# One decoder layer in fp32: the first weights in two transfers, and the last block's mean from row sums of the weights

## The chip, the cores and the metric

The kernel runs on one core of a Trainium2 chip. The metric is the device time in microseconds of one execution, as the median of several runs. A core has TensorE (PE, matrix products), VectorE (DVE), ScalarE (ACT), GpSimd (POOL) and SyncE (SP, which issues most transfers here); sixteen DMA engines move data between the chip's memory and the on-chip buffer.

## The reference, cut to what matters

One decoder layer over 256 positions of width 1024: a wide input projection, block-sparse attention (one block of 256 here, so plain causal attention) and a gated short convolution side by side, an output projection, LayerNorm, a feed-forward part with convolution, LayerNorm again.

```python
proj  = x @ w_in                                   # q | k | v | B | C | h | two gates
y_att = attention(rope(q), rope(k), v) @ w_attn_out
y_cnv = (B * causal_dwconv(C * h)) @ w_conv_out
mix   = (sigmoid(g_att) * y_att + sigmoid(g_cnv) * y_cnv) @ w_o
x     = layer_norm(alpha * x + mix)                # alpha = 2 ** 0.25
u     = causal_dwconv(x @ w_up)                    # width 2 * 2816
f     = (silu(u[..., :2816]) * u[..., 2816:]) @ w_down
x     = layer_norm(alpha * x + f)                  # mean, variance, gain and bias over 1024
```

What matters below is the start of the first product (q, k and v) and the end: the second LayerNorm needs the mean and the variance of each row of `alpha * x + f`, where `f` is a product over 2816 = 22 x 128 rows of `w_down`.

## The kernel before

All products are made in fp32 by splitting each operand into a high part (rounded to the type that PE takes) and a low part (the rest). A product is three matmuls: high by high, high by low and low by high. ACT makes the high parts with a copy (`wh`), DVE the low parts with a subtraction (`wl`). The 128-row groups of the weights are packed by the host into chunks of up to 2048 columns in the order of use; `issue_dma` brings them with SP into three rotating buffers (`raw`), a chunk as a rule in one transfer. `PIECES` says where a chunk is cut into several. A buffer is free again when both parts of its weights are made.

**Head.** Chunk k (of 8) holds 256 columns of x transposed, then the q, k and v weights of one group of 128 input features: 256 + 1024 + 512 columns. Chunk 0 comes in four transfers: x, q weights, k weights, v weights (`PIECES[0]`), chunk 1 in two. While they are under way, PE runs 36 small products of zeros (`warm_up`). Then DVE alone makes the high and the low part of x (L574, L575) and the high part of the q weights (L577), PE runs the products of pass 0 (high by high) and pass 2 (low x by high weights) for each half of the positions, DVE makes the low q weights (L579), and pass 1 follows. The k weights (`split_part(1, 1, 2)`) and the v weights (`split(2)`) follow, each on ACT for the high part and on DVE for the low part. From then on `qkv_split` works ahead by up to two chunks. All matmuls of this stage have line L568.

**Middle.** PE runs through the layer without a break; `slot` places the work of ACT and DVE beside each product by hand: first the ACT steps due, then the high parts of the weights some units ahead (`split_h`, L192), then the low parts (`split_l`, L197), then the DVE steps due. Each engine takes its instructions in the order in which they are written.

**Tail.** `down` adds the product of f group i with its 128 rows of `w_down` to four accumulators `dacc[t][nh]` (two blocks of 128 positions, two halves of 512 columns; L305 to L307). The last 8 of the 22 groups (`TAIL`) are left over to the end. `finish(0)` runs them for block 0, then DVE adds the residual, takes the statistics (`residual`, L779 and L781), and normalises while PE works on block 1. `finish(1)` runs the 8 groups for the first 512 columns of block 1, then for the third and the fourth quarter of the columns each into a bank of its own (`down_part`, bank `e`). Behind the last product come, on DVE: the add of the fourth quarter (L1012), its statistics (L1013), the aggregate over four pieces (L757), the subtraction of the mean and the product with the gain for two halves (L769), and the product with the inverse deviation plus the bias in two pieces of 640 and 384 columns (L766), each with its output transfer (L1025). POOL makes the inverse deviation by a power (L758).

Of the kernel before, what the change touches and what calls it, by code (L numbers as in the profile page):

```python
# [8 lines left out]
F32 = mybir.dt.float32  # L9
# [6 lines left out]
P = 128  # L16
# [35 lines left out]
PIECES = {0: (0, 256, 768, 1280, 1792), 1: (0, 768, 1792)}  # L52
# [85 lines left out]
def layer_kernel(ctx: ExitStack, tc: tile.TileContext, x, wpack, cpack, ln1_g, ln1_b, ln2_g, ln2_b, out):  # L138
# [49 lines left out]
    def split_h(u):  # L188

        issue_dma(units[u]["chunk"] + RAW_BUFS - 1)  # L190
        alloc(u, "h", "wh")
        nc.scalar.activation(units[u]["h"], raw_of(u), AF.Copy)  # L192

# [42 lines left out]
    warm_up(36)  # L236
# [11 lines left out]
    neghalf2 = cst.tile([P, 1], F32, name="neghalf2")  # L248
    invf = cst.tile([P, 8], F32, name="invf")
# [327 lines left out]
    nc.vector.tensor_copy(wh0[:, 0], w0[:, 0])  # L577
    qkv_passes(0, 0, (0, 1), (0, 2))
# [186 lines left out]
    def norm_second(r, mv, ln, cs):  # L765
        nc.vector.scalar_tensor_tensor(r[:, cs], r[:, cs], mv[:, 3:4], ln[:, 1, cs], op0=ALU.mult, op1=ALU.add)  # L766

    def norm_first(r, mv, ln, cs):
        nc.vector.scalar_tensor_tensor(r[:, cs], r[:, cs], mv[:, 0:1], ln[:, 0, cs], op0=ALU.subtract, op1=ALU.mult)  # L769

# [34 lines left out]
    nc.scalar.activation(neghalf2, neghalf, AF.Silu)  # L805
    banks = [acc_bank(f"o1{nh}") for nh in range(2)]
# [185 lines left out]
    def finish(t):  # L992
        r = x1[:, t]
        stats = tmp.tile([P, 4, 6], F32, tag="stats", name=f"rstats{t}", bufs=2)
        if t == 0:
            for k in range(TAIL):
                down(NP - TAIL + k, (t,))
                slot(tail_from + k, take(2))
            assert not pending
            for nh in range(2):  # L1000
                residual(t, nh, dacc[t][nh], x1, r, stats, nh, nh * 512, nh * 512 + 512)
        else:
            for i in range(NP - TAIL, NP):
                down(i, (t,), (0,))
            nc.vector.scalar_tensor_tensor(r[:, 512:1024], x1[:, t, 512:1024], ALPHA, dacc[t][1], op0=ALU.mult, op1=ALU.add)
            for c in range(2):
                residual(t, 0, dacc[t][0], x1, r, stats, c, c * 256, c * 256 + 256)
            for c in range(2, 4):
                bank = ps_pair(f"e{c}")[:, 0]
                for i in range(NP - TAIL, NP):  # L1010
                    down_part(i, bank, c)
                nc.vector.tensor_tensor(r[:, c * 256:c * 256 + 256], r[:, c * 256:c * 256 + 256], bank[:, 0:256], op=ALU.add)  # L1012
                nc.vector.bn_stats(stats[:, c, :], r[:, c * 256:c * 256 + 256])  # L1013
        mv = norm_stats(r, stats, 2 if t == 0 else 4)
        if t == 0:
            for c in range(2):
                cc = slice(c * 512, (c + 1) * 512)
                norm_apply(r[:, cc], r[:, cc], mv, ln2[:, 0, cc], ln2[:, 1, cc])
                nc.sync.dma_start(out[0, t * P:(t + 1) * P, cc], r[:, cc])
            return  # L1020
        for c in range(2):
            norm_first(r, mv, ln2, slice(c * 512, c * 512 + 512))
        for cc, queue in ((slice(0, 640), nc.sync), (slice(640, D), nc.scalar)):
# [3 lines left out]
    for t in range(2):  # L1027
        finish(t)
# [42 lines left out]
```

## Time and profile before

| | |
|---|---|
| time before, median of 3 runs | 365.47 us (365.17 to 365.59) |
| profiled execution, its own time | 366.63 us |
| span of the profiled execution | 364.6 us |
| granted TensorE clock, mean | 0.997 of full |
| busy: PE / PEld / DVE / ACT / POOL | 355.4 / 306.8 / 297.5 / 226.3 / 16.6 us |
| moved between memory and chip | 69.62 MB, mean 191 GB/s |

A row of the timeline reads: start and duration in us, engine, source line, operation, written tile <- read tiles, sizes, number of instructions that the row merges, and in brackets the idle time of the engine ahead of it with what ended it. PEld is the loading of weights into PE, which overlaps its matmuls; SPq and ACTq are the queues of the engines that issue transfers. In a row of groups the numbers behind the bar are the busy time in us and the mean duration of one in ns, then the idle time ahead of the group. In a row of a stretch, each engine has its busy us and, behind x, the number of instructions that touch the stretch, in the order PE, PEld, DVE, ACT, POOL, then clock, DMA share and GB/s. In a row of transfers stand the number, the size and the median us from issue to landing.

### The profile page before, as it was taken

How to read it: one execution, taken by the hardware profiler on the slowest of the kernel's cores; microseconds unless marked ns; L12 is line 12 of the kernel's file. 1: busy time of each engine (PE TensorE's matmuls, PEld its weight loads, DVE VectorE, ACT ScalarE, POOL GpSimd, SP SyncE). 2: the span in 40 equal slices, each digit the busy share in tenths (PEclk: the TensorE clock that was granted, in tenths of full speed). 3: DMA queues.
4: the chain of work that ended last, by engine and by line, in shares of the span. 5: the costliest groups of instructions: out<-in, count | busy, mean ns of one | idle time of the engine just before them, and what ended most of it. 6: DMA issues, size and time to landing. Idle time of an engine off the chain costs nothing.

```text
span 364.6 us, 5227 instructions
## 1 busy us (share of the span) xinstructions
PE 355.4 (97%) x1956; PEld 306.8 (84%) x1956; DVE 297.5 (82%) x514; ACT 226.3 (62%) x392; POOL 16.6 (5%) x38
## 2 busy tenths in 40 slices
PE   8999999999999999999999999999999999999991
PEld 6788888888898888888888888888888888888891
DVE  4787888779795979989769789987968696999884
ACT  3575876577977966653457566765747476777400
POOL 2000000000000113301100000000000000000000
PEclk9999999999999999999999999999999999999998
DMA  8979565435654453787161835548281735653011
GB/s 259 325 254 338 220 236 184 156 115 201 262 192 150 138 214 134 238 320 299 49 231 39 303 124 229 173 172 309 63 322 53 293 108 239 232 230 117 2 58 58
DMA packets 11241, 69.62 MB, mean 191 GB/s; under 512 B 1232, under 2 KB 1616, under 8 KB 4176
## 3 DMA queue, kind: packets, MB, share of 16 engines
q1 hardware_dynamic: 10496, 67.00, 50.3%
q0 software_dynamic: 576, 2.10, 1.7%
q8 instruction: 15, 0.25, 0.3%
q10 hardware_dynamic: 144, 0.20, 0.1%
q14 instruction: 10, 0.08, 0.1%
HBM read 68.24 MB, written 1.05 MB: 190 GB/s over the span
## 4 chain that ended last, share of the span: by engine, by line
PE 96%; DMA 1%; DVE 1%; SPq 0%; ACT 0%; DVEq 0%; issue 0%
PE pb L323 20%; PE pb L330 10%; PE g L323 8%; PE d L305 5%; PE d L306 5%; PE d L307 5%; PE g L330 4%; PE y L323 4%; PE v L568 3%; PE q L568 3%; PE k L568 3%; PE b L323 2%; PE y L330 2%; PE c L323 2%; PE o L305 2%; PE o L307 2%
## 5 line engine op out<-in xcount | busy, mean ns | idle before, releaser
L197 DVE TENSOR_TENSOR wl<-raw,wh 128x1024 fp32r<-128x1024 f32 x99 | 121.0, 1225 | 25.3 <-ACT wh L192 25.1
L192 ACT ACTIVATE wh<-raw 128x1024 fp32r<-128x1024 f32 x99 | 103.7, 1054 | 32.2 <-DMA raw<-in_wpack 32.2
L323 PE MATMUL pb<-x1T,wh 128*128 128x512 f32 x320 | 76.2, 390 | 0.0
L323 PEld LDWEIGHTS pb<-x1T,wh 128*128 128x128 f32 x320 | 59.7, 188 | 12.1
L330 PEld LDWEIGHTS pb<-x1T,wl 128*128 128x128 f32 x320 | 41.0, 191 | 1.6
L330 PE MATMUL pb<-x1T,wl 128*128 128x256 f32 x320 | 41.5, 283 | 0.0
L220 DVE TENSOR_TENSOR wl<-raw,wh 128x1024 fp32r<-128x1024 f32 (+1 forms) x29 | 27.3, 981 | 7.5 <-ACT wh L219 7.3
L323 PE MATMUL g<-xT,wh 128*128 128x512 f32 x128 | 31.7, 395 | 0.0
L305 PE MATMUL d<-wh,f 128*128 128x512 f32 x80 | 31.3, 391 | 0.0
L306 PE MATMUL d<-wl,f 128*128 128x512 f32 x80 | 31.3, 391 | 0.0
L307 PE MATMUL d<-wh,f 128*128 128x512 f32 x80 | 31.1, 389 | 0.0
L219 ACT ACTIVATE wh<-raw 128x1024 fp32r<-128x1024 f32 (+1 forms) x29 | 23.7, 859 | 11.6 <-DMA raw<-in_wpack 7.5
L323 PEld LDWEIGHTS g<-xT,wh 128*128 128x128 f32 x128 | 23.2, 188 | 4.6
L857 DVE SCALAR_TENSOR_TENSOR fc<-fb,consts,fc 128x254 f32<-128x254 f32 x40 | 19.3, 483 | 1.4
L855 DVE SCALAR_TENSOR_TENSOR fc<-fb,consts,fc 128x255 f32<-128x255 f32 x40 | 19.1, 477 | 0.0
L849 ACT ACTIVATE fc<-fb,consts 128x256 f32<-128x256 f32 x40 | 18.0, 497 | 1.4 <-DVE fb L843 1.4
L307 PEld LDWEIGHTS d<-wh,f 128*128 128x128 f32 x80 | 15.0, 188 | 3.2
L305 PEld LDWEIGHTS d<-wh,f 128*128 128x128 f32 x80 | 15.1, 188 | 2.7
L839 ACT ACTIVATE fb<-pb 128x512 f32<-128x512 f32 x20 | 11.8, 592 | 8.7 <-PE pb L330 8.7
L306 PEld LDWEIGHTS d<-wl,f 128*128 128x128 f32 x80 | 15.1, 188 | 2.6
L330 PEld LDWEIGHTS g<-xT,wl 128*128 128x128 f32 x128 | 16.4, 191 | 0.7
L330 PE MATMUL g<-xT,wl 128*128 128x256 f32 x128 | 16.6, 282 | 0.0
(183 smaller groups left out, 580.1 us busy)
## 6 DMA issues: line engine op xcount, KB each, us to landing
raw<-in_wpack SPq DMA_DIRECT2D x55, 1024.0 KB, 5.0
raw<-in_wpack SPq DMA_DIRECT2D x6, 896.0 KB, 6.7
xr<-in_x SPq DMA_DIRECT2D x1, 1024.0 KB, 7.1
ln<-in_ln_g POOLq DMA_DIRECT2D x2, 512.0 KB, 5.7
ln<-in_ln_b POOLq DMA_DIRECT2D x2, 512.0 KB, 6.3
raw<-in_wpack SPq DMA_DIRECT2D x3, 256.0 KB, 3.3
raw<-in_wpack SPq DMA_DIRECT2D x1, 512.0 KB, 6.5
out<-x SPq DMA_DIRECT2D x2, 256.0 KB, 2.0
```

The costliest lines, as they stand in the source:

```text
L192: nc.scalar.activation(units[u]["h"], raw_of(u), AF.Copy)
L197: nc.vector.tensor_tensor(units[u]["l"], raw_of(u), units[u]["h"].bitcast(F32), op=ALU.subtract)
L219: nc.scalar.activation(h, src, AF.Copy)
L220: (eng or nc.vector).tensor_tensor(l, src, h.bitcast(F32), op=ALU.subtract)
L305: nc.tensor.matmul(o, ah, bh, start=start, stop=False)
L306: nc.tensor.matmul(o, ah, bl, start=False, stop=False)
L307: nc.tensor.matmul(o, al, bh, start=False, stop=stop)
L323: nc.tensor.matmul(bank, un["h"][:, k, n0:n0 + P], b[:, k].rearrange("p a s -> p (a s)"), start=k == 0, stop=False)
L330: nc.tensor.matmul(bank[:, 0:S], un["l"][:, k, n0:n0 + P], b[:, k, 0], start=False, stop=k == nk - 1)
L568: nc.tensor.matmul(banks[m][t], (xl if p == 2 else xh)[:, k, t * P:(t + 1) * P], wl if p == 1 else wh, start=k == 0 and p == 0, stop=k == ...
L855: nc.vector.scalar_tensor_tensor(c[:, 1:S], pb[:, a * S:a * S + S - 1], w_ffn(1, j), c[:, 1:S], op0=ALU.mult, op1=ALU.add)
L857: nc.vector.scalar_tensor_tensor(c[:, 2:S], pb[:, a * S:a * S + S - 2], w_ffn(0, j), c[:, 2:S], op0=ALU.mult, op1=ALU.add)
```

## The change

Head: chunk 0 comes in two transfers, x with the q weights (768 columns) and the k with the v weights (1024 columns). The high part of x is made by ACT, at the same time as DVE makes the high q weights; the low part of x follows on DVE. The first products are ordered pass by pass over both halves of the positions. The warm-up has 30 products instead of 36.

Tail: the sum over the columns 768 to 1023 of the last products of block 1 is no longer taken from the products themselves. Each of the last 8 groups of `w_down` gets the sum of its rows over these columns (`rowsum`, an accumulating ACT copy in `split_h`). ACT scales the f groups of block 1 with them (`fs`), POOL adds the eight groups and the two parts up in five steps (`fs_add`; two of them ahead of block 0's power, three behind it), the result is split (`fsr`), and two small products with ones during the fourth quarter (`mean`) sum over the partitions. The other columns are summed by accumulating DVE operations. So the mean is known ahead of the last product. With it ACT squares the first 768 columns (`sq0`, `sq1`), and DVE makes their product with the gain (`res`). Behind the last product come: the add of the fourth quarter to a part from which the mean has been taken, one multiply-and-reduce that completes the variance, the power on POOL beside the product of the last quarter with the gain, and the last operation in two pieces with their output transfers.

```diff
-PIECES = {0: (0, 256, 768, 1280, 1792), 1: (0, 768, 1792)}
+PIECES = {0: (0, 768, 1792), 1: (0, 768, 1792)}
...
+    LAST_UNITS = [U[("dn", i // 2)] + i % 2 for i in range(NP - TAIL, NP)]
+    rowsum = cst.tile([P, TAIL], F32, name="rowsum")
...
         nc.scalar.activation(units[u]["h"], raw_of(u), AF.Copy)
+        if u in LAST_UNITS:
+            j = LAST_UNITS.index(u)
+            nc.scalar.activation(scratch([P, 256], f"rowsum{j}", tag="gs", bufs=3), raw_of(u)[:, 0, 768:1024], AF.Copy,
+                                 accum_out=rowsum[:, j:j + 1])
...
-    warm_up(36)
+    warm_up(30)
...
+    ones32 = cst.tile([P, 2], F32, name="ones32")
+    nc.gpsimd.memset(ones32, 1.0)
+    ones = cst.tile([P, 2], F32R, name="ones")
...
-    nc.vector.tensor_copy(xh[:, 0, :], raws[0][:, 0:S])
+    w0, wh0, wl0 = raw_of(1), units[1]["h"], units[1]["l"]
+    nc.scalar.activation(xh[:, 0, :], raws[0][:, 0:S], AF.Copy)
+    nc.vector.tensor_copy(wh0[:, 0], w0[:, 0])
     nc.vector.tensor_tensor(xl[:, 0, :], raws[0][:, 0:S], xh[:, 0, :].bitcast(F32), op=ALU.subtract)
-    w0, wh0, wl0 = raw_of(1), units[1]["h"], units[1]["l"]
-    nc.vector.tensor_copy(wh0[:, 0], w0[:, 0])
-    qkv_passes(0, 0, (0, 1), (0, 2))
+    for p in (0, 2):
+        qkv_passes(0, 0, (0, 1), (p,))
...
     nc.scalar.activation(neghalf2, neghalf, AF.Silu)
+    nc.scalar.activation(ones, ones32, AF.Copy)
...
-    def finish(t):
...
-    for t in range(2):
-        finish(t)
+    for k in range(TAIL):
+        down(NP - TAIL + k, (0,))
+        slot(tail_from + k, take(2))
...
+    fs = big.tile([P, TAIL, 2, P], F32, tag="d8", name="fs")
+    for j in range(TAIL):
+        nc.scalar.activation(fs[:, j], f_tile(NP - TAIL + j)[:, :, P:2 * P].bitcast(F32), AF.Copy, scale=rowsum[:, j:j + 1])
+
+    def fs_add(a, b):
+        nc.gpsimd.tensor_tensor(a, a, b, op=ALU.add)
+
+    fs_add(fs[:, 0:2], fs[:, 4:6])
+    fs_add(fs[:, 2:4], fs[:, 6:8])
...
+    for nh in range(2):
+        residual(0, nh, dacc[0][nh], x1, r0, stats, nh, nh * 512, nh * 512 + 512)
+    mv = norm_stats(r0, stats, 2)
+    fs_add(fs[:, 0:2], fs[:, 2:4])
+    fs_add(fs[:, 0], fs[:, 1])
+    fs_add(fs[:, 0, 0], fs[:, 0, 1])
+    for c in range(2):
+        cc = slice(c * 512, (c + 1) * 512)
+        norm_apply(r0[:, cc], r0[:, cc], mv, ln2[:, 0, cc], ln2[:, 1, cc])
+        nc.sync.dma_start(out[0, 0:P, cc], r0[:, cc])
...
+    for i in range(NP - TAIL, NP):
+        down(i, (1,), (0,))
+    for c in (1, 2, 0):
+        bank = dacc[1][1][:, 256 * c - 256:256 * c] if c else dacc[1][0]
+        nc.vector.scalar_tensor_tensor(part[c], x1[:, 1, cols3[c]], ALPHA, bank, op0=ALU.mult, op1=ALU.add,
+                                       accum_out=None if c == 1 else sums[:, c:c + 1])
+    fsr = big.tile([P, 2, P], F32R, tag="xT", name="fsr")
+    hl_split(fsr[:, 0], fsr[:, 1], fs[:, 0, 0])
+    bank = ps_pair("e2")[:, 0]
+    for i in range(NP - TAIL, NP):
+        down_part(i, bank, 2)
+    nc.vector.scalar_tensor_tensor(part[1], bank[:, 0:256], 1.0, part[1], op0=ALU.mult, op1=ALU.add, accum_out=sums[:, 1:2])
+    nc.vector.tensor_reduce(sums[:, 3:4], sums[:, 0:3], axis=mybir.AxisListType.X, op=ALU.add)
+    bank = ps_pair("e3")[:, 0]
+    mean = acc_bank("mean")
+    for i in range(NP - TAIL, NP):
+        down_part(i, bank, 3)
+        if i == NP - TAIL + 1:
+            for part_hl in range(2):
+                nc.tensor.matmul(mean[:, 0:2], fsr[:, part_hl], ones, start=part_hl == 0, stop=part_hl == 1)
+
+    for c, f in ((4, -1.0 / D), (5, -1.0 / (32 * D))):
+        nc.vector.tensor_scalar(sums[:, c:c + 1], mean[:, 0:1], sums[:, 3:4], f, op0=ALU.add, op1=ALU.mult)
...
+    for c in range(2):
+        nc.scalar.activation(scratch([P, 512], f"sq{c}")[:, 0:cols3[c].stop - cols3[c].start], part[c], AF.Square,
+                             bias=sums[:, 5:6], scale=1.0 / 32, accum_out=sums[:, 6 + c:7 + c])
+        nc.vector.scalar_tensor_tensor(res[:, cols3[c]], part[c], sums[:, 4:5], ln2[:, 0, cols3[c]], op0=ALU.add, op1=ALU.mult)
+    nc.vector.tensor_scalar(part[2], part[2], sums[:, 4:5], None, op0=ALU.add)
+    nc.vector.tensor_scalar(sums[:, 8:9], sums[:, 6:7], sums[:, 7:8], EPS, op0=ALU.add, op1=ALU.add)
+    nc.vector.tensor_tensor(part[2], part[2], bank[:, 0:256], op=ALU.add)
+    nc.vector.tensor_tensor_reduce(out=scratch([P, 256], "sq2"), in0=part[2], in1=part[2], scale=1.0 / D, scalar=sums[:, 8:9],
+                                   op0=ALU.mult, op1=ALU.add, accum_out=sums[:, 9:10])
+    nc.gpsimd.tensor_tensor(sums[:, 10:11], sums[:, 9:10], neghalf, op=ALU.pow)
+    nc.vector.scalar_tensor_tensor(res[:, cols3[2]], part[2], 1.0, ln2[:, 0, cols3[2]], op0=ALU.mult, op1=ALU.mult)
+    for cc, queue in ((slice(0, 640), nc.sync), (slice(640, D), nc.scalar)):
+        nc.vector.scalar_tensor_tensor(res[:, cc], res[:, cc], sums[:, 10:11], ln2[:, 1, cc], op0=ALU.mult, op1=ALU.add)
+        queue.dma_start(out[0, P:2 * P, cc], res[:, cc])
```

More of the change, by code (lines that the diff above doesn't have):

```diff
@@ L989, in layer_kernel @@
         slot(k, stages)
-    def finish(t):
[L993 to L1023, printed above, removed]
-            norm_second(r, mv, ln2, cc)
-            queue.dma_start(out[0, t * P:(t + 1) * P, cc], r[:, cc])
```

11 lines of the change are left out of this document (7 added, 4 removed).

## The prediction, made before the change was run

> **What bounds the kernel now.** I read the page first: the span, then the chain that ended last, by engine.
>
> ```profile
> span 364.6 us, 5227 instructions
> ...
> PE 96%; DMA 1%; DVE 1%; SPq 0%; ACT 0%; DVEq 0%; issue 0%
> ```
>
> TensorE (PE) is the chain. The profiled execution took 366.63 us against a span of 364.6; the three timed runs lie between 365.17 and 365.59 with a median of 365.47. My sum is a difference, made on the profiled span and then taken from the median. About 0.2% (0.73 us) is what a measurement of this kernel can tell from no change.
>
> Next, the busy time in stretches, and the first 12 us of the timeline.
>
> ```profile
> 10.00:38.60 28.60, 28.60 (x127) 23.66 (x127) 21.05 (x40) 19.25 (x31) 0.00 (x0) 1.00 0.86 310
> 38.60:340.00 301.40, 301.40 (x1682) 261.89 (x1681) 255.75 (x437) 201.80 (x356) 13.56 (x18) 1.00 0.52 189
> ```
>
> ```profile
> 0.74 2.76 SPq L175 DMA_DIRECT2D raw<-in_wpack  x6
> ...
> 0.99 3.44 PE L234 MATMUL warm<-zeros 128*128 128x128 bf16 x36 [0.99 <-DVE zeros L224]
> ...
> 4.04 0.43 DVE L577 CAST wh<-raw 128x512 fp32r<-128x512 f32 x1 [0.46 <-DMA raw<-in_wpack]
> ...
> 4.53 1.19 PE L568 MATMUL q<-wh,xT 128*128 128x512 f32 x4
> 4.97 0.63 ACT L219 ACTIVATE wh<-raw 128x512 fp32r<-128x512 f32 x1 [2.95 <-DMA raw<-in_wpack]
> ...
> 7.20 0.63 ACT L219 ACTIVATE wh<-raw 128x512 fp32r<-128x512 f32 x1 [1.60 <-DMA raw<-in_wpack]
> ...
> 7.88 0.74 PE L568 MATMUL v<-wh,xT 128*128 128x512 f32 x2 [0.29 <-ACT wh L219]
> 8.22 0.42 ACT L219 ACTIVATE xT<-raw 128x256 fp32r<-128x256 f32 x1 [0.39 <-DMA raw<-in_wpack]
> ...
> 9.20 0.69 DVE L220 TENSOR_TENSOR wl<-raw,wh 128x512 fp32r<-128x512 f32 x1
> ...
> 9.94 0.50 PE L568 MATMUL q<-wl,xT 128*128 128x512 f32 x1
> ...
> 11.23 0.39 PE L568 MATMUL k<-wh,xT 128*128 128x512 f32 x1
> ```
>
> From 10.0 to 340 us PE is never idle: 28.60 us of 28.60 for 127 matmuls (0.225 us each), then 301.40 of 301.40. So only what lies ahead of 10 us and behind the last matmul can move the end, and a shift of PE at 10 us is handed on whole if the transfers keep up. The head has gaps. The first product starts at 4.53, 0.06 us behind the cast of the weights (4.04 + 0.43). The value projection (v) starts at 7.88, since its weights landed at 7.20: ScalarE (ACT) had waited 1.60 us for that transfer. The second row block's first low-part product starts at 9.94, because chunk 1 landed at 8.22 and two ACT copies and two VectorE (DVE) subtractions follow it. A measure of the head: the first k product of that row block starts at 11.23; six q products ahead of it put the block's gapless start at 11.23 - 6 x 0.225 = 9.88.
>
> Last, the tail.
>
> ```profile
> 350.88 0.28 PE L305 MATMUL e<-wh,f 128*128 128x256 f32 x1
> ...
> 356.51 0.28 PE L307 MATMUL e<-wh,f 128*128 128x256 f32 x1
> 356.82 0.42 DVE L1012 TENSOR_TENSOR x<-x,e 128x256 f32<-128x256 f32 x1 [1.99 <-PE e L307]
> 357.28 0.43 DVE L1013 BATCH_NORM_STATS2 rstats<-x 128x6 f32<-128x256 f32 x1
> 357.74 0.26 DVE L757 BATCH_NORM_AGGREGATE mv<-rstats 128x2 f32<-128x24 f32 x1
> 358.04 1.44 DVE L769 SCALAR_TENSOR_TENSOR x<-x,mv,ln 128x512 f32<-128x512 f32 x2
> 359.58 1.41 DVE L766 SCALAR_TENSOR_TENSOR x<-x,mv,ln 128x640 f32<-128x640 f32 x2
> ```
>
> ```profile
> 358.08 0.55 POOL L758 TENSOR_TENSOR mv<-mv,neghalf 128x1 f32<-128x1 f32 x1 [9.33 <-DVE mv L757]
> ```
>
> The last quarter-width product ends at about 356.8. Behind it DVE alone works in one row: add, statistics, aggregate, two first-half normalisations (1.44), two second halves (1.41), to 360.99. GpSimd (POOL) takes the power at 358.08 beside that and is waited for by nobody.
>
> **The change, head.** Chunk 0 goes from four transfers to two: 384 KB with the x columns and the q weights, then 512 KB with k and v weights. Six issues take 2.76 us on SP, 0.46 each; four remain, so chunk 1, the constants and chunk 2 are issued 0.92 earlier. Landing times:
>
> ```profile
> raw<-in_wpack SPq DMA_DIRECT2D x1, 512.0 KB, 6.5
> ...
> raw<-in_wpack SPq DMA_DIRECT2D x1, 128.0 KB, 2.1
> ```
>
> ```profile
> 3.00:3.50 0.50, 0.50 (x7) 0.50 (x6) 0.47 (x2) 0.00 (x0) 0.00 (x0) 1.00 1.02 389
> 3.50:4.00 0.50, 0.50 (x11) 0.50 (x9) 0.08 (x1) 0.00 (x0) 0.00 (x0) 1.00 1.11 303
> ```
>
> The first transfer of 128 KB landed 2.1 us after its issue at 0.74. The next half-microseconds moved 389 and 303 GB/s, mean 346. The 384 KB piece has 256 KB (262 kB) more, 0.76 us at that rate: landing at 0.74 + 2.1 + 0.76 = 3.6. Its upper bound is 4.04, when the same bytes had landed in two transfers. Then ACT copies x (0.42) while DVE casts the weights (0.43): both high parts at 4.05. Warm-ups: 11 starts touch 3.5 to 4.0, 0.05 us each, so six fewer end at 4.43 - 0.3 = 4.1. PE starts at about 4.1 instead of 4.53; its low x part comes at 4.5 and the low weights at 5.2, so the six q products end at 5.65.
>
> What decides is the second transfer, T2. At 346 GB/s its 524 kB take 1.52 us: 3.6 + 1.5 = 5.1. The old second piece landed at 4.04 where the same reckoning gives 3.6, 0.44 late, hence 5.55 with that lag. I take 5.3, as now only one transfer stands ahead of it and in the trace the lag grows with the number of transfers. The upper ends: 7.20, where the same 896 KB were complete before, and 7.7, if it takes the 6.5 us of the only 512 KB row from an issue at 1.20.
>
> From T2: high k weights after 0.65 (ACT 0.63 and the hand-over), low ones 0.71 later, four of the six k products behind them (0.90), six v products (1.35): the second row block starts at T2 + 3.6 = 8.9 against 9.88, **0.95 us saved**. Two limits are checked. Chunk 1 must land 1.7 us ahead of that block's low-part product (8.22 to 9.94); it is issued 0.92 earlier, so 7.3, giving 9.0 for that product, which is due at 9.1. Break-even is T2 = 6.25. Moving the two c copies to ACT costs nothing, as ACT idled 2.95 us ahead of 4.97.
>
> **The change, tail.** Added work first. ACT gets eight row sums and eight scaled copies, POOL five adds, PE two mean products, and DVE accumulating forms.
>
> ```profile
> 341.81 0.42 ACT L869 ACTIVATE f<-ff 128x256 fp32r<-128x256 f32 x1 [0.95 <-DVE ff L866]
> ```
>
> ```profile
> L402 DVE CUSTOM_DVE_ANT_0 sm<-s,mask 128x256 f32<-128x256 f32 x8 | 3.1, 419 | 0.0
> ...
> L402 DVE DVE_READ_ACCUMULATOR2_ANT st<- 128x1 f32 x16 | 1.3, 83 | 0.0
> ```
>
> ```profile
> L197 DVE TENSOR_TENSOR wl<-raw,wh 128x1024 fp32r<-128x1024 f32 x99 | 121.0, 1225 | 25.3 <-ACT wh L192 25.1
> ```
>
> ```profile
> 153.18 0.78 POOL L715 TENSOR_TENSOR m<-m 128x256 f32<-128x256 f32 x1 [0.80 <-DVE m L714]
> ...
> 174.36 1.12 POOL L758 TENSOR_TENSOR mv<-mv,neghalf 128x1 f32<-128x1 f32 x1 [9.34 <-DVE mv L757]
> 348.21 0.55 POOL L758 TENSOR_TENSOR mv<-mv,neghalf 128x1 f32<-128x1 f32 x1 [172.72 <-DVE mv L757]
> ```
>
> ```profile
> 153.28 1.76 DVE L197 TENSOR_TENSOR wl<-raw,wh 128x1024 fp32r<-128x1024 f32 x1
> 174.31 0.75 DVE L762 SCALAR_TENSOR_TENSOR x<-xr,mv,ln 128x512 f32<-128x512 f32 x1
> 348.16 0.78 DVE L762 SCALAR_TENSOR_TENSOR x<-x,mv,ln 128x512 f32<-128x512 f32 x1
> 349.04 0.75 DVE L763 SCALAR_TENSOR_TENSOR x<-x,mv,ln 128x512 f32<-128x512 f32 x1
> ...
> 350.49 0.75 DVE L763 SCALAR_TENSOR_TENSOR x<-x,mv,ln 128x512 f32<-128x512 f32 x1
> ```
>
> The row sums (256 elements each, priced like the 0.42 us copy of the same length, plus an accumulator read) sit at one a slot; ahead of the last f tile ACT idles 0.95 us, so that tile is not later. The eight scaled copies follow at about 342.2 and take 8 x 0.42 = 3.4, so the first two POOL adds end before the power of block 0 at 348.21. A 256-element POOL add took 0.78; for 512 elements I estimate 1.3 (between 0.78 and 1.56), for 128 about 0.5. Three adds follow the power: 1.3 + 0.78 + 0.5 = 2.6 us.
>
> These meet block 0's four normalisations (348.16 to 351.24). In the trace the two engines shut each other out: the weight subtraction that began 0.10 us behind a POOL add took 1.76 instead of 1.225, and the power that began 0.05 behind a normalisation took 1.12 instead of 0.55. At 348.21 the power was not held up in the same position, so who wins is not settled. I take turns: each POOL add waits for one normalisation and holds up the next. The power ends at 348.76, before the second normalisation (349.04), so the first add is in the queue ahead of it. DVE then loses about 2.1 of the 2.6 us and ends block 0 at 353.35. If DVE loses nothing, it ends at 351.24 and POOL at about 353.8.
>
> The Trainium skill, "SBUF — State Buffer", section "SBUF: two separate sides", calls the shared port pair an exclusive lock that whichever starts first holds for the whole instruction. By that rule the sum is the one with turns; the rows at 348.16 and 348.21 do not bear it out alone.
>
> With turns: three part sums (0.41, 0.41, 0.68, less overlap, with two accumulator reads of 0.083) take 1.4, the low part of the weighted f sum 0.3, to 355.05. PE wants it at 350.88 + 30 x 0.12 = 354.5 (0.12 is the distance of the 47 steps from 350.88 to 356.51): it stands still for 0.55 us, and two mean products add 0.24. The last product then ends at 357.6. Behind it: add 0.46, square-and-sum 0.45 (0.42 plus part of a read), power with its two hand-overs 0.65, two last operations 1.41: 360.57 against 360.99, **0.4 us saved**. Without the stall the last product ends at 357.05 and the saving is 0.95. The first columns' squares on ACT and their products on DVE lie in the 1.6 us behind the mean and are late only if fsr is. If Square needs another function table, its load falls into the time in which ACT waits for the mean. The two constants of ones are made beside PE work long before. Block 0's output transfers go out later by what DVE loses and stay 9 us ahead of the end. Below the 0.4: if the last power is held up by the 256-element product beside it (0.3 more), 0.1.
>
> Sum: -0.95 - 0.4 = -1.35; 366.63 becomes 365.3, and 365.47 becomes **364.1**.
>
> **The rivals.** *POOL and DVE do not hinder each other in block 0.* For: the power of 0.55 at 348.21. Against: 1.76 and 1.12. Then 365.47 - 0.95 - 0.95 = 363.6. *The second transfer is somewhat late*, T2 about 6.2, so the head gives nothing and only the tail's 0.4 stays: 365.1. For: the old fourth piece was 2.1 us behind the 5.1 of the same reckoning. Against: three transfers stood ahead of it. *The merged transfer makes k and v wait together* (the one that ends slower): before, k had its weights at 4.97 and only v waited for the straggling piece; now both hang on all of the 512 KB. With the 6.5 us of the 512 KB row, T2 = 7.7, the row block starts at 11.3, 1.4 later than now, less 0.4: 366.5. It costs time from T2 = 6.65 on, and over 0.2% from 7.4. Against: that row had five transfers ahead of it. *The clock.* The number of starts per half-microsecond goes from 7 to 11 at about 3.5, so the clock doubles there. The warm-ups began at 0.99, so the doubling took 2.5 us of them. With six fewer it could come later; one more such stretch at half speed costs half of it, 1.25: 365.4.
>
> The Trainium skill, "TensorE: Matmul & The Clock Gate", Part 1, wants about 3.4 us of sustained matmuls for the full clock, which 30 warm-ups (3.1 us) alone do not give; the trace has it after 2.5 us, and real products follow at once, so the chance is small.
>
> **How the numbers follow.** Forecast 364.1: 0.48. No hindrance 363.6: 0.16. T2 somewhat late 365.1: 0.20. k and v wait together 366.5: 0.12. Clock 365.4: 0.04. Faster by over 0.2% holds the first two, 0.64; within 0.2% the third and fifth, 0.24; slower the fourth, 0.12. The likeliest case alone spans 363.7 (T2 at 5.1, power free) to 364.6 (T2 at 5.55, power held up). The range goes from 363.3 (T2 at 5.1, no stall, a little spare) to 365.9, leaving out the merged wait and little else.
>
> **What would show it.** In the new trace: PE's first product at about 4.1; the first k weight copy on ACT at 5.3 (right below 6.2); the first k product of the second row block at about 10.3; POOL adds of 1.3 us between 348 and 353 in the old time frame, with normalisations held up beside them; a PE gap of about half a microsecond inside the last quarter, ahead of the mean products; the last DVE operation about 3.0 us behind the last matmul instead of 4.2. Wrong are: a first k weight copy behind 6.2, no lengthened normalisation, or a new wait of DVE for ACT's squares.

## The result, and the profile after

| | before | changed |
|---|---|---|
| time, median of 14 runs each on one chip | 366.02 us (365.17 to 366.50) | 365.04 us (364.44 to 365.80) |
| profiled execution, own time / span | 366.63 / 364.6 us | 364.5 / 362.7 us |

The ratio is 0.997, with a 95% interval of 0.9961 to 0.9978: faster by 0.98 us, or 0.27%. The two profiles differ by twice that, 2.13 us. The profiled execution of before took longer than any of its 14 timed runs, and that of the changed kernel is among the fastest of its own. So the traces show where time goes, and only the medians show how much of it goes in a usual execution. The page of the changed kernel still has PE as the chain:

```profile
span 362.7 us, 5264 instructions
...
PE 95%; issue 2%; DVE 1%; POOL 1%; POOLq 0%; DVEq 0%
```

The head, from its timeline (the clock's share of it is told further down):

```profile
0.74 1.79 SPq L175 DMA_DIRECT2D raw<-in_wpack  x4
...
0.99 3.32 PE L242 MATMUL warm<-zeros 128*128 128x128 bf16 x30 [0.99 <-DVE zeros L232]
...
3.72 0.42 ACT L586 ACTIVATE xT<-raw 128x256 fp32r<-128x256 f32 x1 [1.70 <-DMA raw<-in_wpack]
3.72 0.43 DVE L587 CAST wh<-raw 128x512 fp32r<-128x512 f32 x1 [2.78 <-DMA raw<-in_wpack]
...
4.29 1.20 PE L579 MATMUL q<-wh,xT 128*128 128x512 f32 x4
...
5.06 1.16 ACT L227 ACTIVATE wh<-raw 128x512 fp32r<-128x512 f32 x2 [0.93 <-DMA raw<-in_wpack]
...
5.72 1.29 DVE L228 TENSOR_TENSOR wl<-raw,wh 128x512 fp32r<-128x512 f32 x2 [0.53 <-ACT wh L227]
...
6.47 0.50 PE L579 MATMUL k<-wl,xT 128*128 128x512 f32 x1
...
7.05 0.42 ACT L227 ACTIVATE xT<-raw 128x256 fp32r<-128x256 f32 x1 [0.84 <-DMA raw<-in_wpack]
...
10.24 0.39 PE L579 MATMUL k<-wh,xT 128*128 128x512 f32 x1
```

Four issues take 1.79 us on SP. The first transfer lands at 3.72, where ACT and DVE start together on its two parts (a landing is read here from the start of the copy that waited for it), the second at 5.06, chunk 1 at 7.05. The first k product of the second row block, the measure of the head, stands at 10.24 instead of 11.23. One wait stands out: the first low-part k product, due 0.2 us earlier, starts at 6.47, behind the subtraction that starts at 5.72.

The tail: block 0's normalisations and the POOL work beside them, then the means and the end.

```profile
343.44 2.54 POOL L1012 TENSOR_TENSOR fs<-fs 128x512 f32<-128x512 f32 x2 [169.53 <-ACT fs L1009]
347.15 0.78 DVE L774 SCALAR_TENSOR_TENSOR x<-x,mv,ln 128x512 f32<-128x512 f32 x1
347.19 0.55 POOL L770 TENSOR_TENSOR mv<-mv,neghalf 128x1 f32<-128x1 f32 x1 [1.21 <-DVE mv L769]
347.71 3.38 POOL L1012 TENSOR_TENSOR fs<-fs 128x512 f32<-128x512 f32 x3
348.03 1.60 DVE L775 SCALAR_TENSOR_TENSOR x<-x,mv,ln 128x512 f32<-128x512 f32 x1
349.55 1.22 DVE L774 SCALAR_TENSOR_TENSOR x<-x,mv,ln 128x512 f32<-128x512 f32 x1
349.86 0.28 PE L316 MATMUL e<-wh,f 128*128 128x256 f32 x1
350.81 0.83 DVE L775 SCALAR_TENSOR_TENSOR x<-x,mv,ln 128x512 f32<-128x512 f32 x1
351.56 0.74 DVE L1038 SCALAR_TENSOR_TENSOR part<-x,d 128x256 f32<-128x256 f32 x2
...
352.84 0.28 DVE L228 TENSOR_TENSOR fsr<-fs,fsr 128x128 fp32r<-128x128 f32 x1
353.45 0.28 PE L1053 MATMUL mean<-ones,fsr 128*128 128x2 f32 x2
...
355.72 0.28 PE L318 MATMUL e<-wh,f 128*128 128x256 f32 x1
356.04 0.42 DVE L1064 TENSOR_TENSOR part<-part,e 128x256 f32<-128x256 f32 x1 [0.33 <-PE e L318]
356.50 0.48 DVE L1065 CUSTOM_DVE_ANT_0 sq<-part,sums 128x256 f32<-128x256 f32 x1
356.90 0.42 DVE L1068 SCALAR_TENSOR_TENSOR res<-part,ln 128x256 f32<-128x256 f32 x1
357.07 0.67 POOL L1067 TENSOR_TENSOR sums<-sums,neghalf 128x1 f32<-128x1 f32 x1 [5.97 <-DVE sums L1065]
357.77 1.41 DVE L1070 SCALAR_TENSOR_TENSOR res<-res,sums,ln 128x640 f32<-128x640 f32 x2 [0.44 <-POOL sums L1067]
```

The four normalisations take from 347.15 to the next operation at 351.56, 4.41 us, where before they took 3.00 (348.16 to 351.16, the next operation there): DVE lost 1.41 us to the three POOL adds, which took 3.38 us.

```profile
351.16 0.68 DVE L1005 SCALAR_TENSOR_TENSOR x<-x,d 128x512 f32<-128x512 f32 x1
```

The low part of the weighted f sum (352.84) is still ready when PE comes to the two mean products at 353.45, so PE does not stop. Behind the start of the last product it is 3.46 us to the end of DVE's work (359.18), where it was 4.48 before (356.51 to 360.99). PE gives 0.23 of this back: its last quarters' products take 5.86 us (349.86 to 355.72) where they took 5.63.

Between the first k product of the second row block and the first `e` product, where the last quarters begin, both traces have 339.6 us, and so have the twelve traces of the experiments (339.62 to 339.66). So what differs between executions lies in the head, in the last quarters with what follows them, and in the way of the output to memory. The 1.9 us between the two spans are 0.99 from the head, 0.79 from the tail and 0.1 behind the last DVE operation.

### The profile page after: what moved, and what is told of

It is laid out like the page before. It is cut to its first block, busy times and chain, and to the rows that moved or that the text cites. A ratio compares the mean times of both kernels' runs of the same rounds, so it can differ in the third digit from the quotient of the medians.

```text
span 362.7 us, 5264 instructions
## 1 busy us (share of the span) xinstructions
PE 355.0 (98%) x1952; PEld 307.2 (85%) x1952; DVE 298.4 (82%) x519; ACT 234.9 (65%) x423; POOL 21.9 (6%) x44
## 4 chain that ended last, share of the span: by engine, by line
PE 95%; issue 2%; DVE 1%; POOL 1%; POOLq 0%; DVEq 0%
PE pb L334 20%; PE pb L341 11%; PE g L334 8%; PE d L316 4%; PE d L317 4%; PE d L318 4%; PE g L341 4%; PE y L334 4%; PE k L579 3%; PE q L579 3%; PE v L579 3%; PE b L334 2%; PE y L341 2%; PE c L334 2%; PE h L334 2%; PE o L318 2%
```

## The experiments

The kernel before ran beside each group of runs on the same chip, with medians of 366.03 to 366.18. The change's own ratio, to be compared, is 0.997.

**One half of the change at a time.** First the head alone:

```diff
 # the kernel before, with of the change only:
+PIECES = {0: (0, 768, 1792), 1: (0, 768, 1792)}
+    warm_up(30)
+    nc.scalar.activation(xh[:, 0, :], raws[0][:, 0:S], AF.Copy)   # and the order of the casts and q passes
```

> The head of the change alone: two transfers for chunk 0, both first high parts at once, passes over both halves, 30 warm-ups; the tail as before. The two traces show the first k product of the second row block at 10.24 instead of 11.23, and everything behind it moved by the same 1.0 us. Theory A (head and tail each give what the traces show): faster than before by 1.0 us, ratio 0.9973. Theory B (the profiled execution of before, 366.63 us against runs of 365.17 to 366.5, had an unusually late landing of its fourth piece, so the head gives little in most runs): 0.2 us or less, ratio 0.9995 or above, and the rest of the measured 1.0 us is the tail's. Theory C (the head gives all, the tail's gain is lost in most runs): ratio 0.997.

Measured: 365.54 us, ratio 0.9989 (0.9975 to 1.0003). Then the tail alone:

```diff
 # the changed kernel, with the head of the kernel before:
-PIECES = {0: (0, 768, 1792), 1: (0, 768, 1792)}
+PIECES = {0: (0, 256, 768, 1280, 1792), 1: (0, 768, 1792)}
-    warm_up(30)
+    warm_up(36)
 # and the casts and q passes in the order of before
```

> The tail of the change alone (row sums, scaled f groups, POOL adds, mean by two small products, one last operation); the head as before. In the two traces the last DVE operation ends 4.18 us behind the start of the fourth quarter's add before and 3.14 behind it after, while two mean products and their neighbours cost PE 0.23: net 0.8 us. Theory A: faster by 0.8 us, ratio 0.9978, and head and tail together 1.8. Theory B: the same 0.8, and with the head's 0.2 the measured 1.0. Theory C: 0.1 us or less, ratio 0.9997. All three expect the power behind the final square-and-sum to take longer than 0.55 and DVE to wait for it.

Measured: 365.67 us, ratio 0.9985 (0.9974 to 0.9996). By the medians each half gives about 0.5 us, and together they make the change's 0.98. The head alone is not shown to be faster: its interval goes from 0.1 us slower to 0.9 faster, and the 0.99 of the traces lies just outside. The tail's interval (0.15 to 0.95 us) holds its 0.79. The timelines, first of the head alone, then of the tail alone:

```profile
5.13 1.15 ACT L219 ACTIVATE wh<-raw 128x512 fp32r<-128x512 f32 x2 [0.81 <-DMA raw<-in_wpack]
...
10.31 0.39 PE L568 MATMUL k<-wh,xT 128*128 128x512 f32 x1
```

```profile
4.79 1.98 PE L579 MATMUL q<-wh,xT 128*128 128x512 f32 x4
6.60 0.63 PE L579 MATMUL q<-wl,xT 128*128 128x512 f32 x2
...
11.28 0.39 PE L579 MATMUL k<-wh,xT 128*128 128x512 f32 x1
```

The head alone shows nearly the same gain in its trace as the full change does (10.31 against 10.24). The second trace has a row that no landing explains: four q products took 1.98 us, where they took 1.20 in the changed kernel's profile.

**The first chunk in four transfers again**, with the rest of the change kept:

```diff
-PIECES = {0: (0, 768, 1792), 1: (0, 768, 1792)}
+PIECES = {0: (0, 256, 768, 1280, 1792), 1: (0, 768, 1792)}
```

> The whole change, but chunk 0 in the four transfers of before. It separates the transfers from the order of the first parts and products. If the merged transfers carry the head's gain (theory A), the k weights land at about 5.0, the v weights at about 7.2 and chunk 1 at about 8.2 as before, and the second row block's first k product is back at 11.1 to 11.3: slower than the whole change by 0.9 to 1.0 us. If it is the order of the first parts and products that carries it, the time stays within 0.2 us of the whole change. Theory B expects the fourth piece to land at about 5.7 in this run and a loss of at most 0.3 us.

Measured: 365.49 us, ratio 0.9984 (0.9971 to 0.9998).

```profile
4.63 1.31 ACT L227 ACTIVATE wh<-raw 128x512 fp32r<-128x512 f32 x2 [1.29 <-DMA raw<-in_wpack]
```

The k weights landed at 4.63, ahead of the change's 5.06, the v weights by 5.31 (the second of the two copies, which take 0.63 each and end at 5.94), and chunk 1 at 6.92; yet the first k product of the second row block came at 10.94, and again the four q products took 2.04 us. Theory A's 7.2 for the v weights failed: in this execution four transfers brought them almost as early as the merged one did, where the first profile of the kernel before had them at 7.20. Theory B's 5.7 is nearer. So this trace does not show what the merging is worth. The medians of the same chip put the four transfers 0.48 behind the change (365.49 against the 365.01 of the next run), between the 0.9 of A and the 0.3 of B, but the intervals overlap, and how the head's gain divides between the transfers and the order of the first products stays open.

**The change once more, unaltered.**

> The changed kernel unaltered, as the measure for the others on the same chip, and as a second trace of its head. Theory A: ratio to before 0.995 to 0.997, second transfer of chunk 0 landed at 5.0 to 5.3, first k product of the second row block at 10.2 to 10.4. Theory B: the same landing, as the merged transfer is not the unusual one. If the runs' spread (364.44 to 365.8) comes from the head's transfers, this trace and the first one differ at that k product by about as much as their own times do; if it comes from the granted clock, they agree there and the 301 us in the middle differ.

Measured: 365.01 us, ratio 0.9972 (0.9959 to 0.9984). The same code gave another trace:

```profile
4.19 2.05 PE L579 MATMUL q<-wh,xT 128*128 128x512 f32 x4
...
5.07 1.15 ACT L227 ACTIVATE wh<-raw 128x512 fp32r<-128x512 f32 x2 [1.04 <-DMA raw<-in_wpack]
...
6.03 0.67 PE L579 MATMUL q<-wl,xT 128*128 128x512 f32 x2
...
10.64 0.39 PE L579 MATMUL k<-wh,xT 128*128 128x512 f32 x1
```

The transfers landed at the same time or earlier (5.07; chunk 1 at 6.67) and PE began 0.1 earlier, but the row block is 0.40 later. The q products start every 0.46 us instead of 0.227: PE ran at half rate until about 6.1. In the kernel before, the profile that the prediction read had the rate double at 3.5. So a second theory (D in what follows) stood against the landing of the transfers (A): the moment at which PE's clock doubles differs between executions. Where it is late, the clock and not a landing sets the new head.

**Taking the last wait away.** The k products pass by pass, so that the low weights are wanted last:

```diff
-    qkv_passes(0, 1, (0, 1), (0, 2, 1))
+    for p in (0, 2, 1):
+        qkv_passes(0, 1, (0, 1), (p,))
```

> The changed kernel, with the k products of the first chunk ordered pass by pass (both high-weight passes of all tiles first, the low-weight pass last) instead of tile by tile, so that TensorE need not wait for the low k weights. If the landing of the second transfer sets the head (theory A), the wait of 0.43 us ahead of the first low-weight k product in the changed kernel's profile goes, the first k product of the second row block comes at about 9.9 instead of 10.24, and the time falls by 0.3 to 0.4 us, to a ratio of about 0.996 to the kernel before. If in most executions the moment at which the clock doubles sets the head (theory D), as in the second profile of the changed kernel where q products ran at half rate up to 5.5 us and no product waited for weights, the order does nothing there: first k product of the second block at 10.5 to 10.7 when the clock doubles late, and the median moves by less than 0.15 us.

Measured: 365.16 us, ratio 0.9965 (0.9954 to 0.9977): no difference from the change that can be told. In the trace the first products ran at half rate to 6.4 and no product behind the first one waited for a weight; the row block's first k product is at 10.96, as the clock theory had it.

**The k weights apart from the v weights.**

```diff
-PIECES = {0: (0, 768, 1792), 1: (0, 768, 1792)}
+PIECES = {0: (0, 768, 1280, 1792), 1: (0, 768, 1792)}
```

> The changed kernel with its first chunk in three transfers: x columns with q weights as in the change, then k and v weights apart, so one issue of 0.46 us more. Theory A: the k weights land at about 4.4 to 4.6 instead of 5.06 and the v weights at about 5.3; chunk 1 lands 0.3 to 0.5 us later, at about 7.2 to 7.5, which its low-part product (1.7 us later) still bears; the first k product of the second row block comes at 9.8 to 10.2 and the time falls by 0 to 0.3 us. Theory D: q products at half rate up to about 5.5 us fill the time in either case, so the earlier k weights bring nothing; the time is the same within 0.15 us, or up to 0.3 worse if chunk 1 is late.

Measured: 365.02 us, ratio 0.9971 (0.9961 to 0.9981), the change's own. The k weights landed at 4.50 and the v weights at 6.06, the latter later than both together did in the change (5.06); no product waited; the k product came at 10.21, with the clock doubling at about 5.3.

**The warm-ups.** First 36 of them:

```diff
-    warm_up(30)
+    warm_up(36)
```

> The changed kernel with 36 warm-up products instead of 30. At half rate 36 end at about 4.9 to 5.0 where 30 end at 4.3 or a little later; with the clock doubled at 3.5, as in the profile of the kernel before, they end at 4.4. Theory D, with the clock's doubling not tied to the number of warm-ups: the first product comes 0.1 to 0.7 us later, q products then run at full rate more often, the first k product of the second block is 0 to 0.4 us later and the time 0 to 0.4 us longer. Rival (the clock doubles late because the six warm-ups are missing and TensorE is idle or unevenly busy behind them): with 36 the doubling comes by 4.0 to 4.5 us in the profile and the time is 0.1 to 0.4 us shorter than with 30.

Measured: 365.11 us, ratio 0.9972 (0.9961 to 0.9983). The 36 ran at half rate to about 4.8, the q products still took 1.88 us, and the k product was at 11.07. In this execution six more warm-ups did not bring the doubling forward to the 4.0 to 4.5 of the rival, and the median is no shorter; the rival with the missing warm-ups has nothing on its side. Then only one:

```diff
-    warm_up(30)
+    warm_up(1)
```

> The changed kernel with one warm-up product instead of 30, so that TensorE idles from about 1.1 us to its first product at about 4.1. If the doubling of the clock needs some microseconds of products ahead of it (2.5 in the profile of before, 4 to 5.5 in most others): the first products run at half rate until 6.5 to 9 us, the six q, six k and six v products and some of the next block take 0.45 us each, the first k product of the second row block comes at 11.5 to 13 us and the time rises by 1 to 2.5 us to 366 to 367.5. If the clock doubles at a moment that has nothing to do with TensorE's work: doubling at 4.5 to 6.6 as with 30 warm-ups, first k product at 10.2 to 11.1, time unchanged within 0.2 us.

Measured: 366.28 us, ratio 1.0002 (0.9992 to 1.0012). The loss against the change, about 1.2 us, is as large as all that the change gained.

```profile
4.42 2.05 PE L579 MATMUL q<-wh,xT 128*128 128x512 f32 x4 [3.14 <-DVE wh L587]
6.26 1.05 PE L579 MATMUL q<-wl,xT 128*128 128x512 f32 x2
7.12 1.05 PE L579 MATMUL k<-wh,xT 128*128 128x512 f32 x2
...
12.27 0.39 PE L579 MATMUL k<-wh,xT 128*128 128x512 f32 x1
```

Now half rate lasts to about 9.2, 4.8 us behind the first product, where no other profile has it beyond 6.9. So the doubling follows PE's own work, after a time that differs.

**The kernel before once more.**

> The kernel before, unaltered, once more, for a third profile of the old head. Theory D (the moment at which TensorE's clock doubles differs between executions, 3.5 us in the first profile of before, 5.3 to 6.6 in most others): the doubling is somewhere between 3.5 and 6.6 us, and the first k product of the second row block stays at 11.1 to 11.4 in either case, since chunk 1 lands at about 8.2 and sets it; so the old head does not feel the late clock, while the new one, at 10.2 to 11.1, does. Theory A (landing alone): the same 11.1 to 11.4, and the doubling has no bearing. From the last quarter's first product to the last DVE operation's end it takes 10.1 us as before. Ratio 1.000 within 0.0012.

Measured: 366.42 us, ratio 1.0003 (0.9994 to 1.0013).

```profile
6.77 0.63 ACT L219 ACTIVATE wh<-raw 128x512 fp32r<-128x512 f32 x1 [1.50 <-DMA raw<-in_wpack]
...
10.72 0.39 PE L568 MATMUL k<-wh,xT 128*128 128x512 f32 x1
```

The expectation failed in one number: the k product came at 10.72 and not at 11.1 to 11.4, since the v weights landed at 6.77 and chunk 1 at 7.73. So the landings, too, differ between executions: in the three traces of the old head the v weights landed at 7.20, 6.30 and 6.77, and with the same four transfers under the new order by 5.31. The profile that the prediction started from has the latest of the four. The clock doubled early, near 3.6; and the tail was as ever.

**Both orders in one kernel**, the last two head edits together:

> The changed kernel with the first chunk in three transfers and the k products pass by pass, both edits of the two runs that did either one alone. Theory A (landings set the head): with k weights at about 4.5 and no wait for their low part, the head gains over either alone: first k product of the second row block at 9.8 to 10.0, time 0.2 to 0.4 us under the change's. Theory D: from its first product on TensorE has no idle time left ahead of the second row block, so that block comes at the first product's start plus 18 products plus half of what lies ahead of the doubling of the clock: first k product at 10.2 (clock at 5.3) to 10.9 (clock at 6.4), time within 0.2 us of the change's, ratio 0.996 to 0.998.

Measured: 364.61 us (363.99 to 365.75), ratio 0.9962 (0.9945 to 0.998). It is the lowest median of all, 0.4 under the change, but its interval holds the change's 0.997, so it is not shown to be faster than the change.

```profile
4.13 1.40 PE L579 MATMUL q<-wh,xT 128*128 128x512 f32 x4
5.37 0.62 PE L579 MATMUL q<-wl,xT 128*128 128x512 f32 x2
5.82 1.07 PE L579 MATMUL k<-wh,xT 128*128 128x512 f32 x4
...
9.90 0.39 PE L579 MATMUL k<-wh,xT 128*128 128x512 f32 x1
```

Here PE has no gap from 4.13 on, and the sum is open to view. Four products at full rate take 1.07, at half rate 2.05; a row in between tells when the rate doubled, at the first start plus twice the excess over 1.07, here 4.8. Where all four are slow, the rows behind them tell it in the same way. From the first q product to the first k product of the second row block stand 24 products of 0.227 us, 5.45 in all, plus half of the time at half rate:

| run | first q product | clock doubles at about | without a gap | first k product, measured |
|---|---|---|---|---|
| both orders | 4.13 | 4.8 | 9.91 | 9.90 |
| three transfers | 4.18 | 5.3 | 10.21 | 10.21 |
| the change again | 4.19 | 6.1 | 10.61 | 10.64 |
| four transfers | 4.38 | 6.5 | 10.90 | 10.94 |
| k pass by pass | 4.57 | 6.4 | 10.94 | 10.96 |
| 36 warm-ups | 4.77 | 6.4 | 11.03 | 11.07 |
| adds on VectorE | 4.45 | 6.9 | 11.10 | 11.13 |
| one warm-up | 4.42 | 9.2 | 12.25 | 12.27 |
| the change, first profile | 4.29 | 4.6 | 9.87 | 10.24 |
| the head alone | 4.48 | 4.7 | 10.03 | 10.31 |
| more work on POOL | 4.23 | 5.5 | 10.30 | 10.98 |
| the tail alone (old head) | 4.79 | 6.6 | 11.15 | 11.28 |
| before, first profile | 4.53 | 3.6 | 9.98 | 11.23 |
| before again | 4.26 | 3.6 | 9.71 | 10.72 |

The sum is bookkeeping: it takes the rate from the first rows, so it shows that PE had no gap and not why the rate doubled when it did. The run with both orders does not tell the theories apart, since A's 9.8 to 10.0 and the sum with the clock at 4.8 are the same. The upper eight have no wait for weights behind the first product, and the sum meets them to 0.04 us. The others are above it by their waits: 0.3 to 0.4 in the change's head with an early clock, 0.7 where the second transfer landed at 5.81 (more work on POOL), 1.0 to 1.25 in the old head with an early clock, and only 0.1 there with a late one. So the head is worth 0.4 to 1.0 us between two executions with an early clock (10.72 and 11.23 against 10.24 and 10.31), and the less, the later the clock of the new one: half rate fills the time in which PE used to wait. Over the five profiles with the change's own head the k product lies between 10.24 and 11.13, with 10.64 in the middle; the three of the old head have 11.23 in the middle. The difference is 0.6, near the 0.56 by which the median of the head alone lies under that of before. The sum and the rows show the mechanism. How much of the shortfall of the medians comes from the late clock, and how much from the v weights of the old head landing earlier than at 7.20 in other executions (theory B), is not shown by so few profiles.

**More work on POOL.** Two more adds of 512 elements ahead of the three:

```diff
     mv = norm_stats(r0, stats, 2)
+    for _ in range(2):
+        fs_add(fs[:, 4:6], fs[:, 6:8])
     fs_add(fs[:, 0:2], fs[:, 2:4])
```

> The changed kernel with two more additions of 512 elements a partition on GpSimd, on columns that nobody reads afterwards, ahead of the three that make the weighted f sum. In the changed kernel's profile the sum is ready about 0.35 us before TensorE wants it. Theory (the contention is there but hidden by 0.35 us of slack): two adds of 1.27 us alone, up to 1.6 with turns taken, put the weighted sum at 355.0 to 356.0 instead of 352.8, TensorE stands still for 1.6 to 2.6 us ahead of the mean products, unless the three part sums are held up with it; the time rises by 1.6 to 2.6 us, to 366.6 to 367.6. Rival (the weighted sum has over 2 us of spare time, and another wait sets the tail): the time stays within 0.3 us.

Measured: 366.50 us, ratio 1.0004 (0.9995 to 1.0012): 1.2 us slower than the change by the ratios, 1.5 by the medians, under the expected 1.6 to 2.6.

```profile
348.48 6.46 POOL L1012 TENSOR_TENSOR fs<-fs 128x512 f32<-128x512 f32 x5
348.80 1.60 DVE L775 SCALAR_TENSOR_TENSOR x<-x,mv,ln 128x512 f32<-128x512 f32 x1
350.32 1.77 DVE L774 SCALAR_TENSOR_TENSOR x<-x,mv,ln 128x512 f32<-128x512 f32 x1
352.13 1.67 DVE L775 SCALAR_TENSOR_TENSOR x<-x,mv,ln 128x512 f32<-128x512 f32 x1
...
355.33 0.60 PE L1055 MATMUL mean<-ones,fsr 128*128 128x2 f32 x2 [0.95 <-ACT fsr L227]
```

Each of the three normalisations beside the adds takes over twice its 0.75, and POOL takes 6.46 us for adds that would take about 5.1 alone (three of 1.27, which is half of the 2.54 at 343.44, and by the prediction's prices one of 0.78 and one of about 0.5). One by one, the three long adds (1.37 us from 348.48, 1.62 from 349.93, 1.74 from 351.50) end at 349.85, 351.55 and 353.24, and the three normalisations at 350.40, 352.09 and 353.80: each normalisation ends 0.54 to 0.56 behind an add, and each further add 1.15 behind a normalisation, so the two engines take turns. PE stands still for 0.95 us ahead of the mean products, which now take 0.46 instead of 0.15, as the second waits for the low part, which ends at 355.60: the last quarters take 7.27 us instead of 5.86, 1.41 more, which accounts for the measured loss. So the stall that the prediction described exists, and the change is just on this side of it.

**The adds on VectorE.**

```diff
     def fs_add(a, b):
-        nc.gpsimd.tensor_tensor(a, a, b, op=ALU.add)
+        nc.vector.tensor_tensor(a, a, b, op=ALU.add)
```

> The changed kernel with all five additions of the weighted f sum on VectorE instead of GpSimd. The first two (512 elements) run while VectorE has nothing due; the last three take 0.7 + 0.4 + 0.3 = 1.4 us of its own queue, where in the changed kernel the turns with GpSimd cost it the same 1.4 us. So the normalisations return to 0.78 to 0.83 us each, the weighted sum is ready at the same moment within 0.3 us, and the time is the same within 0.2 us. Rival (the exclusion by GpSimd costs more than doing the work on VectorE, and its slack of 0.35 us is used up in many executions): 0.2 to 0.5 us faster.

Measured: 365.14 us, ratio 0.9963 (0.995 to 0.9976): no difference from the change that can be told.

```profile
344.30 1.50 DVE L1012 TENSOR_TENSOR fs<-fs 128x512 f32<-128x512 f32 x2 [1.41 <-ACT fs L1009]
...
348.79 1.42 DVE L1012 TENSOR_TENSOR fs<-fs 128x512 f32<-128x512 f32 x3
...
354.72 0.27 PE L1053 MATMUL mean<-ones,fsr 128*128 128x2 f32 x1 [0.19 <-DVE fsr L228]
```

The last three adds take 1.42 us of DVE's time, what the turns with POOL cost it in the change (1.41). The first two were not free, though, as the expectation had them: DVE reached them at 344.30, after ACT's copies, and the residual behind them was late. The weighted sum came late, and PE's last quarters took 6.21 us, 0.35 more than in the change. The median of the five runs does not show these 0.35 us; the intervals (a gain of 0.8 to 1.4 us for the change, of 0.9 to 1.8 here) leave room for them.

## Why the prediction was right or wrong

**The sign and the size.** A gain of 1.35 us was forecast, 0.98 measured (0.8 to 1.4 by the interval). The time came out at 365.04 instead of 364.1 for a further reason: the three runs of before that the forecast started from (365.17 to 365.59) lie at the low end of its 14 (365.17 to 366.50, median 366.02). That is 0.55 of the 0.94; the other 0.37 is the gain.

**Landings: right.** First transfer 3.6 forecast, 3.72 in the profile (3.53 to 3.99 over the runs); second 5.3, 5.06 in the profile (5.06 to 5.81 where k and v come together); chunk 1 7.3, 7.05. The rival with a merged wait, T2 at 7.7, did not come, and neither did 6.2.

**The head's 0.95: right in the profile (0.99), in part by luck, and too large for the median (about 0.5, between -0.1 and 0.9).** In the profile two misses cancel: T2 came at 5.06, 0.24 early, and from T2 to the second row block's first product it took 3.82 (to 8.88) and not 3.6. For the median, the step that failed is the start of PE "at about 4.1" with six q products of 0.225 us behind it, by which T2 alone sets the row block. It takes the doubling at 3.5 from the one trace at hand and holds it for every execution. In the change's profile the landing at 3.72 and 30 warm-ups at half rate throughout (3.32 us) put the first product at 4.29 and not at 4.1, and in most others half rate lasted to 5.3 or later. The clock was among the rivals, at 1.25 us, for the wrong reason (six warm-ups fewer) and with a chance of 0.04. In fact the lateness is there with 36 as well, it is the common case, and the new head's k product lies up to 0.9 us later with it (10.24 to 11.13). The second weak point is the base: the 9.88 from which the 0.95 is counted comes from the profile with the latest v weights (7.20); the kernel before once more had its k product 0.51 earlier. Which of the two took more from the median stays open. The Trainium skill, "TensorE: Matmul & The Clock Gate", Part 1, says that the window in which activity is judged runs freely and that the number of slow products differs between runs of one kernel. These traces agree, with a doubling 2.6 to 5.9 us behind the first warm-up at 0.99 wherever there were 30 or 36; their spread is wider than the 500 ns to either side that the Trainium skill gives there. The prediction quoted that part's 3.4 us and left this sentence out.

**The turns of POOL and DVE: right in kind, too large.** Forecast: DVE loses 2.1 us; measured 1.41. The three adds in a row met only three of the four normalisations, with 0.85, 0.47 and 0.08 lost (1.60, 1.22 and 0.83 against 0.75). The exclusive lock of the Trainium skill's "SBUF — State Buffer", section "SBUF: two separate sides", is borne out here by these rows and by the alternating ends in the run with five adds; the rows of before alone had left it open.

**The stall of 0.55: wrong, mainly for that reason.** The step that failed is the 2.1 us that DVE was to lose. With 0.7 less lost, and with the part sums and the low part taking 1.5 us and not 1.7, the low part of the weighted sum was ready about 0.3 us before PE wanted it. With two more adds PE did stand still, for 0.95 us. The two mean products cost the 0.24 forecast (0.23).

**Behind the last product: 2.97 forecast for the steps, 3.14 measured** (356.04 to 359.18). The power took 0.67 from 357.07, beside the product of 256 elements that had begun at 356.90; the held-up power was in the range, at 0.3, and cost 0.12. Squares on ACT were not late. Together the tail gave 0.79 in the traces, between the 0.4 forecast and the 0.95 without the stall. In every trace of the new tail the time from the first `e` product to the end of DVE's work is 9.31 to 9.33 us, in all three of the old one 10.11 or 10.12, apart from the two runs that altered the adds. So the traces give the tail its 0.8 us in every execution that they show, and of the change's 0.98 that would leave the head 0.2; the run with the head alone gives it 0.56 and the run with the tail alone gives the tail 0.43. The intervals allow either, and how the 0.98 divides is not settled.

## What to carry to other kernels

Before a gap at the start of a kernel is priced from one trace, read the rate of the first products in several executions: a clock that doubles late fills the gap with slow products, and a transfer that lands earlier then buys less. Take the landing times of the old kernel from several executions as well. When work is moved to an engine that shuts another one out, count for the other engine only those of its operations that fall beside it, and ask how much spare time the chain behind has; here 0.3 us decided between no stall and one of a microsecond.

## What the runs showed that was not expected

The clock's doubling lay between 3.6 and 6.9 us in kernels whose warm-ups all began at 0.99, without any sign in the granted-clock column: the stretch from 3.00 to 3.50 in the prediction, at half rate, has 1.00 as well. By the medians thirty warm-ups against one are worth about 1.2 us, more than either half of the change. What lies behind the last DVE operation, the output's way to memory, took between 3.15 and 3.92 us with the same two transfers, a spread of 0.8 us that follows none of the edits.
